# An encoder block on one core: rotary keys third among the column tiles, early sums of wo on ScalarE, and thirty products of zeros ahead of the last four

## The chip, the core and the metric

The kernel runs on one core of a Trainium2 chip. A core has TensorE (PE, matrix products into PSUM), VectorE (DVE), ScalarE (ACT), GpSimd (POOL) and SyncE (SP, which here issues nearly all DMAs). The metric is device time in microseconds, the median of several runs. One execution was also recorded by the hardware profiler; times inside the kernel come from that record and count from its first instruction.

## What is computed

One layer: a projection `x @ w_in` into eight groups of columns, two kinds of attention, a gate, an output projection, and LayerNorm on the residual. Cut to what matters:

```python
def reference(x, w_in, rel_pos_bias, sink_logits, w_out, ln_gain, ln_bias):   # x: (1, 1024, 1024) float32
    h = jnp.einsum('bsd,de->bse', x, w_in[layer])                             # 2688 columns
    q_a, k_a, v_a, z_a, q_b, k_b, v_b, z_b = jnp.split(h, SPLIT_POINTS, axis=-1)
    y_a = neighborhood_attention(q_a, k_a, v_a, rel_pos_bias[layer])          # 8 heads of 64, window 8 x 16
    y_b = windowed_gqa_with_sink(rotary(q_b), rotary(k_b), v_b, sink_logits[layer])   # 8 query, 2 key heads, |i-j| <= 128
    mixed = jnp.concatenate([y_a * jax.nn.silu(z_a), y_b * jax.nn.silu(z_b)], axis=-1)
    y = jnp.einsum('bse,ed->bsd', mixed, w_out[layer])
    x = layer_norm(DEEPNORM_ALPHA * x + y, ln_gain[layer], ln_bias[layer])
```

## The kernel before

Products of float32 matrices are formed from float16 parts: each operand is scaled by a power of two and split into a high and a low part, and three products (high x high, high x low, low x high) go into one PSUM bank. The scale of a matrix comes from sums of absolute values.

The work has four stages, and the order of all instructions is written out by the program itself (a manual schedule), so each engine's queue is exactly in program order.

1. **Values.** The value columns are projected first (L537), while `x` and the value weights arrive.
2. **Prologue of column tiles.** The other 21 tiles of 128 columns of `w_in` are named in `ORDER` (L30): `zb*` and `z*` are gates, `kb` the rotary keys, `qb*` rotary queries, `k*`, `q*` the other attention. `project(name)` runs two groups of 24 products (L430), one for each half of the 1024 tokens, each into one of two PSUM banks tagged `pj`. A group may start when the bank's last reader, two groups before, is done. After a group comes `evac`. The first six tiles (`NPRO`) are projected in a block, 288 products counted by `ran`; steps behind a group are hung at a count of products (`after=`, `at(...)`). For a rotary tile these are: a copy to `rp_raw` on ACT (L364), a shuffle, two products and a sum on DVE (L365 to L368), high parts on ACT (L300), low parts on DVE (L306), and for keys copies on POOL (L347). For the first three names of `ORDER` a gate's SiLU is one ACT instruction (L391); later gates take a tanh on ACT (L394) and a step on DVE (L395). Beside this stand the sums over the columns of the other 15 tiles (`sum_w`, L755, L757). `w_scale` turns sums into scales with a small product on PE (L266) and a chain of small DVE steps; its last call, at product 217, uses the sums of all 15.
3. **Attention loop.** 128 units, one a step: scores on PE (L860, L861), a biased minimum on DVE (L870), exp on ACT (L885), a split into high and low parts on ACT and DVE (L895, L896), a transposing DMA issued by SP (L899), and products with the values (L925). The remaining 15 tiles and then parts of the output projection fill PE between the scores (`FILL_AT`). Other work is put on ACT, DVE or POOL by a planner: each operation has a priority and a cost in us for each engine that may take it, `due` books the work of an engine, and an engine takes an operation where its booked work leaves room before the next step. The sums of `wo` (`wo_scan`, L968 on ACT or L970 on DVE) are such operations: 16 of them, through four buffers, so that the load of each waits for the sum four before. The first four are placed in the prologue on ACT, the others are queued at the steps in `SCAN_LD` (0, 2, 4, 6, ...). When all are done, `wo_scale` forms the scale of `wo` at a step from 24 on that is a multiple of four.
4. **Output projection and LayerNorm** (`final`). Eight blocks of 128 rows; products at L1178, sums into the residual and statistics on DVE (L1213, L1219). The last block ends in `norm_last`: part of its normalisation is done by PE, with `identf` times the bias first (L1243), then, when the row's scale is known, two diagonal matrices `dr` and `dn` made by ACT (L1248, L1249) times the row and the gain (L1250, L1251). At float32 each of these is recorded as two products.

Of the kernel before, what the change touches and what calls it, by code (L numbers as in the profile page):

```python
# [26 lines left out]
QSCALE = 2.0 ** -15  # L27
LTT, LPP, BH, ND, NA, NX, F1 = 1, 6, 9, 1, 1, 8, 0.2
NSPLIT, NP = 6, 2
ORDER = ["zb0", "z0", "zb1", "kb", "qb0", "z1", "qb1", "zb2", "qb2", "k0", "qb3", "zb3", "q0", "k1", "q1",  # L30
         "k2", "q2", "k3", "q3", "z2", "z3"]
NPRO = 6
NS = 21 - NPRO
NR = 5
FILL = ORDER[NPRO:]
FILL_AT = [0, 8, 17, 25, 33, 41, 49, 57, 66, 74, 82, 90, 98, 106, 113, 121, 123.5, 126, 128, 131, 136]
# [29 lines left out]
def hybrid_block(ctx, tc, xT, x, wt, wv, wo, bias, sink, gain, lbias, cos, sin, bmask, out):  # L66
    nc = tc.nc
# [10 lines left out]
    def bank(tag):  # L78
        bufs = {"pj": 2, "s": 4, "t": 2}[tag]
        return (ps1 if bufs == 1 else ps2).tile([128, 512], F32, tag=tag, name=f"ps_{tag}", bufs=bufs)  # L80
# [19 lines left out]
    def zslot(name, tag="z"):  # L100
        return zp.tile([128, S], F32, tag=tag, name=name, bufs=3 if tag == "z" else 1)
# [15 lines left out]
    invt = const.tile([128, 2], F32, name="invt")  # L117
    NT = len(ORDER)
    unit = const.tile([128, 2], F32, name="unit")
# [11 lines left out]
    warm = const.tile([128, 128], F16, name="warm")  # L131
# [17 lines left out]
    clock = {"step": None}  # L149
# [19 lines left out]
    def enq(eng, fn, *deps, prio=1, after=0, cost=None):  # L169
        op = Op(eng, fn, deps, prio, cost)  # L170
        if clock["step"] is not None:
            queues[eng].append(op)
        elif after:
            events.setdefault(ran[0] + after, []).append(op.emit)
        else:
            op.emit()
        return op
# [44 lines left out]

    NH = 2 * len(ORDER)
    NL = NH - 2 * NR
# [37 lines left out]
    def w_scale(n):  # L262
# [8 lines left out]
        nc.vector.tensor_scalar(v, g, xrs, 0.5, op0=ALU.mult, op1=ALU.mult)  # L271
        nk, nq = ORDER.index("kb"), ORDER.index("qb0")
        if n >= NPRO - 1:
# [60 lines left out]
    def split_k(p, half, src, dep=None):  # L334
        col = dep is None
        ops, high = [], []
        prio = 0 if dep is None else 1
        eng = "pool" if dep and clock["step"] is not None else "dve"
        for j in range(2):
            a, o = slice(64 * j, 64 * j + 64), slice(64 - 64 * j, 128 - 64 * j)  # L340
            hi, lo = split_hl(lambda j=j, a=a: place(own("kh", p, j), a, half, col),
                              lambda j=j, a=a: place(own("kl", p, j), a, half, col),
                              taken_from(src, a, col), dep is None, eng)

            def dup_(w, j=j, a=a, o=o):
                t = own(w, p, j)
                nc.gpsimd.tensor_copy(place(t, o, half, col), place(t, a, half, col))  # L347

            high.append((enq("act", hi, dep, prio=prio, after=28 if dep else 0), lo, dup_))
        for j, (o1, lo, dup_) in enumerate(high):  # L350
            o2 = enq(eng, lo, *([o1] if dep else [h[0] for h in high]), prio=prio, after=32 if dep else 0)
            ops.append(o2)
            dup = [enq("pool", lambda d=dup_: d("kh"), o1, after=32 if dep else 0, cost=0.62),
                   enq("pool", lambda d=dup_: d("kl"), o2, after=36 if dep else 0, cost=0.62)]
            stk_ops.setdefault((p, j, half), []).extend(dup)
        return ops

    def rope(ps, half):
        live = clock["step"] is not None
        sl = slice(512 * half, 512 * half + 512)  # L360
        eng, mul = ("pool", nc.gpsimd) if live else ("dve", nc.vector)
        raw = tiles["ap"].tile([128, 1024], F32, tag="va", name="rp_raw", bufs=6)[:, :512]
        sw = tiles["ap"].tile([128, 1024], F32, tag="va", name="rp_sw", bufs=6)[:, :512]
        o1 = enq("act", lambda: nc.scalar.activation(raw, ps, AF.Copy, scale=QSCALE), prio=0)  # L364
        o2 = enq("dve", lambda: nc.vector.stream_shuffle(sw, raw, SWAP), o1, after=2)  # L365
        o3 = enq(eng, lambda: mul.tensor_mul(raw, raw, tiles["cos"][:, sl]), o2, after=3)
        o4 = enq(eng, lambda: mul.tensor_mul(sw, sw, tiles["sin"][:, sl]), o2, after=3)
        o5 = enq(eng, lambda: mul.tensor_add(raw, raw, sw), o3, o4, after=4)  # L368
        return raw, o1, o5

    def evac(name, half, ps):
        sl = slice(512 * half, 512 * half + 512)
        kind = name.rstrip("0123")
        p = int(name[-1]) if name[-1].isdigit() else 0
        n = ORDER.index(name)
        if kind in ("kb", "qb"):
            raw, o1, o5 = rope(ps, half)
            if kind == "kb":
                split_k("b", half, raw, o5)
            else:  # L380
                split_q(f"b{p}", half, raw, o5)
            return [o1]
        if kind == "k":
            return split_k(p, half, ps)
        if kind == "q":
            return split_q(p, half, ps)
        e = 4 + p if kind == "zb" else p
        if half == 0:
            zt[e] = zslot(f"z{e}", ZTAG.get(name, "z"))
        if name in ORDER[:3]:  # L390
            nc.scalar.activation(zt[e][:, sl], ps, AF.Silu, scale=inv[:, n:n + 1])  # L391
            return []
        half_inv = invt[:, 0:1] if n < NPRO else invt[:, 1:2]
        o = enq("act", lambda: nc.scalar.activation(zt[e][:, sl], ps, AF.Tanh, scale=half_inv), prio=0)  # L394
        o2 = enq("dve", lambda: nc.vector.scalar_tensor_tensor(  # L395
            zt[e][:, sl], zt[e][:, sl], 1.0, ps, op0=ALU.add, op1=ALU.mult), o, prio=0)
        stk_ops.setdefault(name, []).append(o2)
        return [o2]
# [565 lines left out]
    def wo_scan(i, b):  # L964
        def scan(eng):
            m = wom[:, 4 * i + b:4 * i + b + 1]
            if eng == "act":
                nc.scalar.activation(junk2, wor[:, b], AF.Abs, accum_out=m)  # L968
            else:
                nc.vector.tensor_reduce(m, wor[:, b], axis=mybir.AxisListType.X, op=ALU.add, apply_absolute_value=True)  # L970

        scans.append(enq("any", scan, load_ops["wor", i, b], prio=1.9,
                         cost={"act": 0.85, "dve": 0.68} if clock["step"] is not None else {"act": 0.85}))

    for n in range(NSCAN):
        at(190 + 6 * n, wo_load, SCAN[n // 4], n % 4)
        at(222 + 8 * n, wo_scan, SCAN[n // 4], n % 4)
# [217 lines left out]
    def final():  # L1195
# [25 lines left out]
        def row_stats(t):  # L1221
            mv = fp.tile([128, 2], F32, tag="mv", name="mv")
            nc.vector.bn_aggr(mv, stats[t][:, :8 if t == 3 else 2, :])
            sd = fp.tile([128, 1], F32, tag="sd", name="sd")
            nc.scalar.activation(sd, mv[:, 1:2], AF.Sqrt, bias=eps)
            return mv, sd
# [13 lines left out]
        def norm_last(t):  # L1240
            ts = slice(128 * t, 128 * t + 128)
            xr = xrs[t]
            nc.tensor.matmul(pn[:, :WP], identf, bb[:, HP], start=True, stop=False)  # L1243
            mv, sd = row_stats(t)
            nc.vector.scalar_tensor_tensor(xr[:, H0], xr[:, H0], mv[:, 0:1], gb[:, H0], op0=ALU.subtract, op1=ALU.mult)
            rstd, nmr = row_scale(mv, sd)
            dr, dn = (fp.tile([128, 128], F32, name=n, bufs=1) for n in ("dr", "dn"))
            nc.scalar.activation(dr, identf, AF.Copy, scale=rstd)  # L1248
            nc.scalar.activation(dn, identf, AF.Copy, scale=nmr)  # L1249
            nc.tensor.matmul(pn[:, :WP], dr, xr[:, HP], start=False, stop=False)  # L1250
            nc.tensor.matmul(pn[:, :WP], dn, gb[:, HP], start=False, stop=True)  # L1251
            nc.vector.scalar_tensor_tensor(xr[:, H1], xr[:, H1], mv[:, 0:1], gb[:, H1], op0=ALU.subtract, op1=ALU.mult)
            nc.scalar.copy(xr[:, HP], pn[:, :WP])
            for h in (H0, H1):
                nc.vector.scalar_tensor_tensor(xr[:, h], xr[:, h], rstd, bb[:, h], op0=ALU.mult, op1=ALU.add)
                nc.sync.dma_start(out[ts, h], xr[:, h])
            nc.scalar.dma_start(out[ts, HP], xr[:, HP])
# [121 lines left out]
    for i in range(-LD, NU + LO):  # L1379
# [9 lines left out]
        if i in SCAN_LD:  # L1389
            n, b = divmod(NSCAN + SCAN_LD.index(i), 4)  # L1390
            wo_load(SCAN[n], b, *scans[-4:-3])
            wo_scan(SCAN[n], b)
# [7 lines left out]
        if i in B_LD:  # L1400
            n = B_LD.index(i)
# [145 lines left out]
```

## Time and profile before

| | |
|---|---|
| median of three runs | 446.61 us (445.05 to 447.45) |
| profiled execution | 444.73 us, its span 442.9 us |
| PE busy | 431.9 us, 97% of the span |
| DVE, ACT, POOL busy | 333.6, 313.7, 280.5 us |
| mean granted PE clock | 0.994 |

The span runs from the first to the last instruction; the execution's own time has some work of start and end around it. Busy times are unions of the recorded durations. A product is recorded for longer than the pipeline needs it, so rows of PE overlap: the distance from start to start tells the rate.

### The profile page before, as it was taken

The page shows a single profiled execution, that of the slowest core. Times are in us where ns is not written, and L with a number is a line of the kernel's source. Part 1 is how long each engine was busy: PE and PEld are TensorE (multiplying, and loading weights), DVE is VectorE, ACT ScalarE, POOL GpSimd, SP SyncE. Part 2 cuts the span into 40 slices and gives each one's busy share as a digit, 9 for nine tenths or more (in the row PEclk, how much of TensorE's full clock was granted, in tenths as well). Part 3 has the DMA queues.
Part 4 walks back from the last instruction along what each step waited for, and adds up shares of the span by engine and source line. Part 5 has one row for each costly group of instructions (what it writes and reads, how often), then busy time and mean ns, then how long its engine had stood idle before and what let it go on. Part 6 is the DMA issues. An engine that isn't in the chain of part 4 may idle for free.

```text
span 442.9 us, 9338 instructions
## 1 busy us (share of the span) xinstructions
PE 431.9 (97%) x3205; PEld 251.3 (57%) x3205; DVE 333.6 (75%) x821; ACT 313.7 (71%) x660; POOL 280.5 (63%) x299
## 2 busy tenths in 40 slices
PE   8999999999999999999999999999999999999992
PEld 7997754444445555565555565656556565444451
DVE  5978967519988898888888977878778756665554
ACT  5749789759678888888988969788788753342221
POOL 0120074535848647779998799798989871077681
PEclk9999999999999999999999999999999999999997
DMA  7922469995138999985969999999799979612122
GB/s 255 406 95 60 132 234 337 259 308 161 48 96 184 188 195 186 206 162 123 179 137 214 194 198 210 225 185 187 141 199 228 154 130 385 252 47 96 47 91 100
DMA packets 128815, 80.12 MB, mean 181 GB/s; under 512 B 97280, under 2 KB 106368, under 8 KB 128768
## 3 DMA queue, kind: packets, MB, share of 16 engines
q1 hardware_dynamic: 128624, 79.40, 74.5%
q8 instruction: 25, 0.41, 0.4%
q14 instruction: 22, 0.18, 0.1%
q10 hardware_dynamic: 144, 0.13, 0.1%
HBM read 48.01 MB, written 8.42 MB: 127 GB/s over the span
## 4 chain that ended last, share of the span: by engine, by line
PE 80%; DMA 6%; DVE 5%; issue 3%; POOL 2%; ACT 1%; SPq 1%; POOLq 0%; DVEq 0%; ACTq 0%
PE ps_pj L430 35%; PE ps_s L1178 9%; PE ps_t L925 7%; PE ps_s L537 6%; PE ps_pj L1178 4%; PE ps_s L860 4%; PE ps_s L861 4%; DMA vd<-vt 3%; PE ps_pj L537 3%; PE ps_t L537 3%; PE ps_t L1178 2%; DMA ws<-in_wt 2%; PE ps_t L948 2%; POOL wl L246 1%; DMA wvraw<-in_wv 1%
## 5 line engine op out<-in xcount | busy, mean ns | idle before, releaser
L430 PE MATMUL ps_pj<-xf,wh 128*128 128x512 f16 x672 | 201.3, 379 | 1.1 <-DVE z L395 1.1
L430 PE MATMUL ps_pj<-xf,wl 128*128 128x512 f16 x336 | 127.3, 379 | 0.0
L430 PEld LDWEIGHTS <-wh 128*128 128x128 f16 x672 | 63.7, 98 | 61.0 <-issue 1.3
L885 ACT ACTIVATE ps_s<-sn,nm 128x385 f32<-128x385 f32 (+3 forms) x128 | 70.9, 554 | 32.5 <-DVE nm L870 32.2
L896 DVE SCALAR_TENSOR_TENSOR split<-ps_s,split 128x384 f16<-128x384 f32 (+1 forms) x128 | 66.8, 522 | 19.3 <-ACT split L895 17.7
L245 POOL TENSOR_SCALAR wr<-wr,wsc 128x512 f32<-128x512 f32 x32 | 23.8, 744 | 65.2 <-ACT wh L240 56.1
L895 ACT ACTIVATE split<-ps_s 128x384 f16<-128x384 f32 (+1 forms) x128 | 58.2, 454 | 1.6
L430 PEld LDWEIGHTS <-wl 128*128 128x128 f16 x336 | 32.8, 98 | 38.1
L870 DVE CUSTOM_DVE_ANT_0 sn<-ps_s,bias,sg 128x368 f32<-128x368 f32 (+1 forms) x64 | 36.2, 566 | 13.8 <-PE ps_s L861 13.8
L870 DVE CUSTOM_DVE_ANT_0 sn<-ps_s,bm,nsk 128x384 f32<-128x384 f32 (+1 forms) x64 | 40.7, 636 | 2.4 <-PE ps_s L861 2.2
L246 POOL TENSOR_TENSOR wl<-wr,wh 128x512 f16<-128x512 f32 x32 | 39.6, 1238 | 2.7
L860 PE MATMUL ps_s<-ks,qs 128*128 128x384 f16 (+2 forms) x128 | 39.7, 310 | 0.0
L861 PE MATMUL ps_s<-ks,qs 128*128 128x384 f16 (+2 forms) x128 | 39.7, 310 | 0.0
L925 PEld LDWEIGHTS <-tr 128*128 128x128 f16 (+1 forms) x1056 | 36.2, 98 | 2.4
L1178 PEld LDWEIGHTS <-A 128*128 128x128 f16 x216 | 20.1, 98 | 20.7
L347 POOL COPY ks<-ks 64x512 f16<-64x512 f16 x40 | 26.5, 662 | 5.8 <-DVE ks L306 1.8
L1213 DVE SCALAR_TENSOR_TENSOR xr<-ps_s,yc,xr 128x512 f32<-128x512 f32 (+1 forms) x22 | 16.0, 727 | 14.5 <-PE ps_s L1178 14.0
L1281 ACT ACTIVATE xr<-xr,nmr,rstd 128x1024 f32<-128x1024 f32 x6 | 7.4, 1240 | 27.0 <-POOL nmr L1232 27.0
L240 ACT ACTIVATE wh<-wr,wsc 128x512 f16<-128x512 f32 x32 | 22.8, 712 | 0.7 <-DVE wsc L270 0.7
L1178 PEld LDWEIGHTS <-m 128*128 128x128 f16 x144 | 13.9, 98 | 15.8
L537 PEld LDWEIGHTS <-xf 128*128 128x128 f16 x192 | 18.6, 98 | 7.2
L1283 POOL TENSOR_TENSOR xr<-xr,gb 128x512 f32<-128x512 f32 x13 | 16.8, 1290 | 8.3 <-ACT xr L1281 8.1
(214 smaller groups left out, 892.3 us busy)
## 6 DMA issues: line engine op xcount, KB each, us to landing
wr<-in_wt SPq DMA_DIRECT2D x32, 256.0 KB, 3.6
ws<-in_wt SPq DMA_DIRECT2D x15, 512.0 KB, 7.2
wor<-in_wo SPq DMA_DIRECT2D x20, 256.0 KB, 3.8
xr<-in_x SPq DMA_DIRECT2D x8, 512.0 KB, 10.6
out<-xr SPq DMA_DIRECT2D x15, 256.0 KB, 2.0
wob<-in_wo SPq DMA_DIRECT2D x14, 256.0 KB, 3.8
bias<-in_bias SPq DMA_DIRECT2D x8, 440.0 KB, 4.4
wvraw<-in_wv SPq DMA_DIRECT2D x9, 320.0 KB, 5.7
```

The lines of the kernel that those rows point to most:

```text
L246: nc.gpsimd.tensor_sub(l, raw, h)
L347: nc.gpsimd.tensor_copy(place(t, o, half, col), place(t, a, half, col))
L430: nc.tensor.matmul(ps, a[:, k % 4, :], mv, start=(k == 0 and i == 0), stop=(k == KT - 1 and i == 2))
L537: nc.tensor.matmul(ps[:, :320], lh[:, ts], rh[:, cs], start=(k == ko[0] and i == 0), stop=(k == ko[-1] and i == 2))
L860: nc.tensor.matmul(ps[:, :n], q, sl[0], start=True, stop=False)
L861: nc.tensor.matmul(ps[:, :n], q, sl[1], start=False, stop=True)
L870: nc.vector.tensor_tensor_reduce(sn[:, :n], ps[:, :n], bias_t, sg[:, c:c + 1], init, op0=ALU.add, op1=ALU.min, accum_out=nm)
L885: nc.scalar.activation(pt[:, :m], sn[:, :m], AF.Exp, bias=nm, scale=-1.0, accum_out=acc)
L895: nc.scalar.activation(hl[:, :m, 0, :], src, AF.Copy, scale=PSCALE)
L896: nc.vector.scalar_tensor_tensor(hl[:, :m, 1, :], src, PSCALE, hl[:, :m, 0, :], op0=ALU.mult, op1=ALU.subtract)
L925: nc.tensor.matmul(ps[:, w * m:w * m + e], a, b_, start=(i == 0), stop=(i == len(mms) - 1))
L1178: nc.tensor.matmul(ps[:, cs], lh[:, 128 * t:128 * t + 128], rh[:, cs], start=(fresh and e == 0 and n == 0), stop=(e == len(terms) - 1 and ...
```

## The change

Three edits. The rotary keys `kb` change places with the gate tile `zb1`; the condition for the SiLU form of a gate becomes its index below 4, so that `zb1` in fourth place keeps it. The sums of `wo` that are queued at the loop's steps 0, 2 and 4 may go to ACT alone; before, every sum queued inside the loop could go to ACT or DVE. In `norm_last`, thirty products of a 128 x 128 float16 tile of zeros with itself, into a bank that nothing reads, are put on PE between the product with the bias and the four that wait for `dr` and `dn`.

```diff
-ORDER = ["zb0", "z0", "zb1", "kb", "qb0", "z1", "qb1", "zb2", "qb2", "k0", "qb3", "zb3", "q0", "k1", "q1",
+ORDER = ["zb0", "z0", "kb", "zb1", "qb0", "z1", "qb1", "zb2", "qb2", "k0", "qb3", "zb3", "q0", "k1", "q1",
          "k2", "q2", "k3", "q3", "z2", "z3"]
...
-        if name in ORDER[:3]:
+        if n < 4:
             nc.scalar.activation(zt[e][:, sl], ps, AF.Silu, scale=inv[:, n:n + 1])
             return []
...
         scans.append(enq("any", scan, load_ops["wor", i, b], prio=1.9,
-                         cost={"act": 0.85, "dve": 0.68} if clock["step"] is not None else {"act": 0.85}))
+                         cost={"act": 0.85, "dve": 0.68} if (clock["step"] or 0) > 4 else {"act": 0.85}))
...
             nc.tensor.matmul(pn[:, :WP], identf, bb[:, HP], start=True, stop=False)
+            busy = bank("s")
+            for _ in range(30):
+                nc.tensor.matmul(busy[:, :128], warm, warm, start=True, stop=True)
             mv, sd = row_stats(t)
```

## The prediction

> **What bounds the kernel now.** I read the page first (shares, the clock row, the chain), then the waits of TensorE (PE), then the timeline around each wait.
>
> ```profile
> span 442.9 us, 9338 instructions
> ...
> PE 431.9 (97%) x3205; PEld 251.3 (57%) x3205; DVE 333.6 (75%) x821; ACT 313.7 (71%) x660; POOL 280.5 (63%) x299
> ...
> PE 80%; DMA 6%; DVE 5%; issue 3%; POOL 2%; ACT 1%; SPq 1%; POOLq 0%; DVEq 0%; ACTq 0%
> ```
>
> PE is busy for 431.9 of 442.9 us, and the chain that ended last is 80% PE. So a change can only pay where PE waits, and can only cost where it makes PE wait or gives it more work on the path. The waits of PE are four (who waited for whom: us in total, times, longest):
>
> ```profile
> PE ps_t L1250 <- ACT dr L1248: 2.7, 1, 2.7
> PE ps_pj L430 <- DVE z L395: 1.1, 1, 1.1
> PE ps_t L463 <- DVE warm L132: 1.0, 1, 1.0
> PE ps_pj L537 <- ACT wvh L493: 0.7, 1, 0.7
> ```
>
> The last two lie at the start, which the diff does not touch. The second is the hand-over from the prologue (six column tiles) to the attention loop, where the order of tiles matters. The first is the wait in `norm_last`, where the thirty products go. Everything from 123.5 us to the last rows is one unbroken stream of PE, so the sums of wo have no PE wait to remove.
>
> **Part 1: rotary keys third instead of fourth.** The wait that it can touch, in the timeline (start, us taken, engine, line, what, and in brackets the idle time before it and who ended it):
>
> ```profile
> 122.04 0.27 PE L860 MATMUL ps_s<-ks,qs 128*128 128x256 f16 x1
> ...
> 122.15 0.27 PE L861 MATMUL ps_s<-ks,qs 128*128 128x256 f16 x1
> ...
> 122.78 0.69 DVE L395 SCALAR_TENSOR_TENSOR z<-z,ps_pj 128x512 f32<-128x512 f32 x1
> ...
> 123.52 0.59 PE L430 MATMUL ps_pj<-xf,wh 128*128 128x512 f16 x2 [1.10 <-DVE z L395]
> ```
>
> PE wants the accumulator bank of z1's first half; VectorE (DVE) reads it at L395 only until 123.47. Counted from start to start, L861 is followed after 1.37 us, where L860 was followed after 0.11: the wait costs 1.26 us. L395 is late because DVE's queue ahead of it has no gap from 109.63 on:
>
> ```profile
> 107.79 1.81 DVE L306 TENSOR_TENSOR ks<-rp_raw,ks 64x512 f16<-64x512 f32 x2
> 109.63 0.17 DVE L267 TENSOR_REDUCE wg<-ps_t 128x1 f32<-128x15 f32 x1
> ...
> 111.97 0.73 DVE L365 STREAM_SHUFFLE rp_sw<-rp_raw 128x512 f32<-128x512 f32 x1
> ...
> 115.39 1.40 DVE L306 TENSOR_TENSOR ks<-rp_raw,ks 64x512 f16<-64x512 f32 x2
> ...
> 116.82 0.73 DVE L365 STREAM_SHUFFLE rp_sw<-rp_raw 128x512 f32<-128x512 f32 x1
> ...
> 120.12 2.63 DVE L306 TENSOR_TENSOR qs<-rp_raw,qs 64x512 f16<-64x512 f32 x2
> ```
>
> The two `ks` rows are the low parts of kb, the tile that moves. All of kb's steps hang at fixed counts of products behind its own two groups (shuffle 2, products 3, sum 4, high parts 28, low parts 32, copies 32 and 36), so they all move with it by one tile: 48 products, some 10.4 us at the 0.216 us of this stream (starts at 123.52 and, two products on, 123.95). That takes the 1.40 us out of the queue directly ahead of L395: 123.47 becomes 122.07, just ahead of the 122.26 at which PE could go on. The 1.81 us also leaves, so the scale chain at 109.63 need not start that late: it waits only for PE's row at 106.69 (below), and the rotary work behind it, of 3.4 and 3.3 us, only for PE's groups. L395 can then run as early as its tanh allows, and the wait goes with room to spare. What replaces kb in fourth place is zb1, whose evacuation is one ScalarE (ACT) SiLU per half and nothing on DVE or POOL; with `n < 4` it keeps that SiLU. **Minus 1.26 us.**
>
> What does kb's new place collide with? Its high parts (four casts on ACT), its copies (POOL) and its rotary steps (DVE) now stand among the last sums over w's columns, and PE itself waits for these sums: the small product L266 stands in PE's own queue, so everything behind it would wait too.
>
> ```profile
> 95.98 1.06 ACT L755 ACTIVATE junk<-ws 128x1024 bf16<-128x1024 f32 x1 [3.58 <-DMA ws<-in_wt]
> ...
> 103.14 0.72 ACT L240 ACTIVATE wh<-wr,wsc 128x512 f16<-128x512 f32 x1 [0.70 <-DVE wsc L270]
> ...
> 105.89 0.19 ACT L755 ACTIVATION_READ_ACCUMULATOR junk<-ws 128x1 f32 x1
> ```
> ```profile
> 106.69 0.17 PE L266 MATMUL ps_t<-wm,ones 128*128 128x15 bf16 x1
> ```
> ```profile
> L300 ACT CAST ks<-rp_raw 64x512 f16<-64x512 f32 x4 | 2.4, 610 | 0.1
> L364 ACT ACTIVATE rp_raw<-ps_pj 128x512 f32<-128x512 f32 x4 | 2.3, 581 | 0.0
> L391 ACT ACTIVATE z<-ps_pj,inv 128x512 f32<-128x512 f32 x2 | 1.4, 687 | 1.5 <-PE ps_pj L430 1.4
> ```
>
> (The last three are groups: busy us, mean ns of one.) The last sum ends at 106.08, PE comes at 106.69: 0.61 us of room. In program order all four casts now come ahead of it. The first two (about 1.2 us) fall into the 3.58 us in which ACT waits for a load. The other two add 2 x 0.61 = 1.22; two SiLU in place of two copies to rp_raw add 2 x 0.106 = 0.21; the 0.70 us at L240 goes, since DVE no longer has kb's first rotary ahead of that scale. Net 0.73 us later, so PE waits 0.12. Ends: 0 (all hidden) and, with all four casts and both SiLU in full and the 0.70 kept, 2.44 + 0.21 - 0.61 = 2.04. I take 0.12, because the gap of 3.58 us is three times what is put into it. **Plus 0.12 us.**
>
> The other users of kb come later than before relative to it: the first scores at 122.04 only find their keys earlier. rp_raw and rp_sw lie over tiles of the value weights, with which the prologue is done long before, so they wait for nothing; SP's queue is passed by none of kb's steps, since kb issues no DMA of its own.
>
> **Part 2: sums 4 to 6 of wo on ACT alone.** The rows of these sums:
>
> ```profile
> L968 ACT ACTIVATE junk<-wor x10: 612/622/630, 109.6 to 194.6; 128x512 bf16<-128x512 f32 x10
> L968 ACT ACTIVATION_READ_ACCUMULATOR junk<-wor x10: 186/188/192, 110.2 to 195.2; 128x1 f32 x10
> ...
> L970 DVE TENSOR_REDUCE wom<-wor x6: 679/684/687, 143.1 to 174.4; 128x1 f32<-128x512 f32 x6
> ```
> ```profile
> ACT ps_s L885 <- DVE nm L870: 10.8, 13, 2.1
> ```
>
> Each group has its fewest, middle and most ns, and the first and last start. DVE's first two (from 143.1) are sums 4 and 5 (of 0 to 15), queued at steps 0 and 2; sum 6 is on ACT already. So two of 0.684 leave DVE and two of 0.62 + 0.19 = 0.81 enter ACT, which from 120 to 200 us waits 10.8 us for DVE: ACT has the room, DVE gains what ACT was waiting for. PE does not wait in this stretch, so the direct gain is 0. A sum that slips holds back the load of the sum four later (same buffer) and behind it SP's queue; the sums 8 and 9 are queued four steps after 6 and more, so I expect them, and the scale of wo, at the same steps. **0 us**; ends: minus 0, since nothing waits, and plus 1.6 (both sums in full on PE's path).
>
> **Part 3: thirty products in the wait.**
>
> ```profile
> 431.90 0.50 PE L1178 MATMUL ps_s<-wo,z 128*128 128x128 f16 x6
> ...
> 432.91 0.65 PE L1243 MATMUL ps_t<-bb,identf 128*128 128x256 f32 x2
> 436.27 0.67 PE L1250 MATMUL ps_t<-xr,dr 128*128 128x256 f32 x2 [2.71 <-ACT dr L1248]
> 436.78 0.59 PE L1251 MATMUL ps_t<-gb,dn 128*128 128x256 f32 x2
> ```
> The stretch after them, by windows (length, busy of PE, its weight loads, DVE, ACT and POOL, the granted clock, DMA), and the first products of the program:
>
> ```profile
> 434.30:437.70 3.40, 1.10 (x4) 0.68 (x4) 3.15 (x8) 0.99 (x3) 0.00 (x0) 1.00 0.20 77
> 437.70:441.00 3.30, 0.00 (x0) 0.00 (x0) 0.00 (x0) 0.37 (x1) 0.00 (x0) 0.50 0.40 150
> ```
> ```profile
> 0.99 2.95 PE L463 MATMUL ps_t<-warm 128*128 128x128 f16 x26 [0.99 <-DVE warm L132]
> ```
>
> Six 128-wide f16 products take 0.50 us, from 431.90 to 432.24 start to start, or 0.056 each. Thirty take 1.7 us, from about 433.4 to 435.1, and `dr` releases PE at 436.27: they lie wholly inside the wait, with 1.1 us left. Their bank is one that the third row block used and DVE has long read. At the slow rate of the first 26 (2.95 us, about 0.107 each) they would take 3.2 and overrun by 0.3 to 0.5; PE comes from a full-clock stream, so I leave that out. In this profile the granted clock was 1.00 up to 437.70: the last four products already ran at full clock, and all that is left to save is the refill of the first (0.67 us for the first two, 0.59 for the last two): **minus 0.08 us.** But the clock fell to 0.50 at 437.70, right behind a stretch of 3.40 us of which 1.10 were busy. A run in which such a boundary lies 1 to 2 us earlier would run these four products at half rate.
>
> The Trainium skill, "TensorE: Matmul & The Clock Gate", Part 1 (The HAM clock gate), says that the clock halves after a window of about 3.4 us that was idle, and that the windows run freely, not with the kernel. By that rule read strictly, a wait of 2.7 us holds no whole idle window and the zeros are worth nothing in any run: the sum would lose no term but the chance of the first rival below. The trace disagrees with the strict reading: the stretch ahead of the fall was a third busy.
>
> **The sum.** Minus 1.26, plus 0.12, plus 0, minus 0.08: minus 1.22 us. The profiled execution took 444.73 us (its span of 442.9 and 1.83 around it), so it would take 443.5. The median of the runs before, 446.61 (445.05 to 447.45), lies 1.88 above it; the same 1.22 taken from it gives **445.4 us**, 0.27% faster, inside the 0.5% that a measurement of this kernel can tell from no change.
>
> **The rivals.**
>
> *The clock falls in the wait in most runs.* The profile is faster than all three timed runs; in those the boundary may lie inside the wait, and the last four products then take about twice as long, as the first 26 of the program do beside those of L1178 (0.107 against 0.056). One of the four takes some 0.215 (0.59 for two, less the 0.38 for which one lasts): 4 x 0.215 = 0.86 us, straight on the path to the last output. The zeros end that. Time: 446.61 - 1.22 - 0.86 = 444.5. For it: the fall behind a window one third busy. Against it: of 3.4 us of possible positions only some 1.5 hit the four products.
>
> *Slower: the sums over w wait behind kb's casts.* If the load of the tenth sum comes earlier, or the rotary work later, so that the casts miss the gap of 3.58 us, PE waits 2.04 us at L266. The wait at L395 goes all the same, so the time is 446.61 + 2.04 - 1.26 - 0.08 = 447.3. It turns from gain to loss when the last sum ends later than 106.69 + 1.34 = 108.0 us.
>
> *The gain is given back inside attention.* PE comes 1.2 us earlier to every tile that it reads; where a transposed tile lands shortly before use, PE waits instead, and the two sums on ACT push exp, split and transfer back by up to 1.6. Then 446.6, no change. For it:
>
> ```profile
> 266.65 2.69 SPq L899 DMA_TRANSPOSE tr<-split  x2
> ```
> ```profile
> 271.02 0.85 PE L925 MATMUL ps_t<-va,tr 128*128 128x64 f16 x22
> ```
> ```profile
> tr<-split SPq DMA_TRANSPOSE x128, 3.6
> ```
>
> PE reads such tiles 4.4 us after the issue, and landing takes a median of 3.6. Against it: the front of the pipeline starts earlier too, as DVE is rid of its backlog at 123.
>
> **How the numbers follow.** Forecast 0.45, clock rival 0.30, given back 0.14, slower rival 0.11. The runs of before differ by 2.4 us, so a new median may lie 1 us off. The bound for faster is 444.38: the clock rival is beyond it 7 times in 10 at most with that scatter and a somewhat larger saving (0.21), the forecast 4 times in 10 (0.18), the others hardly (0.01): 0.40. The bound for slower is 448.84: the slower rival with the scatter, or an order that the planner changes further on: 0.10. That leaves 0.50. The range goes from the clock rival less the scatter, 443.3, to the slower rival, 447.4.
>
> **What would show it.** Right: no PE wait for L395; kb's casts ahead of 95.98; DVE's scale chain at 107 instead of 109.6; L266 at most 0.3 late; no sum of wo on DVE before 150; thirty products of 0.056 and a wait for `dr` of about 1.1. Wrong: PE waits at L266 of over 1 us, new waits for `tr` at L925 or for banks at L860, the scale of wo a step of four later, or thirty products at 0.107.

## The result, and the profile after

Median of 11 runs: 442.56 us (441.67 to 444.87), against 446.11 us (444.57 to 447.48) for 11 runs of the kernel before on the same chip. The ratio is 0.993, with a 95% interval of 0.9913 to 0.9947: 3.1 us faster by the ratio (3.55 by the two medians), where 1.2 were forecast, and below the forecast range. The profiled execution took 441.67 us.

The page of the changed kernel:

```profile
span 439.9 us, 9401 instructions
...
PE 433.5 (99%) x3235; PEld 253.7 (58%) x3235; DVE 335.0 (76%) x820; ACT 314.2 (71%) x662; POOL 279.4 (64%) x299
...
PE 97%; DVE 2%; ACT 0%; issue 0%; DVEq 0%; ACTq 0%
```

The thirty products are the thirty more on PE; ACT has two records more and DVE one fewer. The chain that ended last was 80% PE, with 6% of DMA and 5% of DVE; now it is 97% PE. The waits of PE (who for whom: us in total, times, longest):

```profile
PE ps_t L1253 <- ACT dr L1251: 1.3, 1, 1.3
PE ps_t L463 <- DVE warm L132: 1.0, 1, 1.0
```

The wait for DVE's L395 is gone, and no new one has come. The wait for `dr` is 1.3 because zeros fill the rest. (From L1243 on, line numbers are three higher.)

The hand-over to the loop, in the timeline of the changed kernel:

```profile
118.95 0.69 DVE L395 SCALAR_TENSOR_TENSOR z<-z,ps_pj 128x512 f32<-128x512 f32 x1
...
121.48 0.27 PE L861 MATMUL ps_s<-ks,qs 128*128 128x256 f16 x1
121.59 0.59 PE L430 MATMUL ps_pj<-xf,wh 128*128 128x512 f16 x2
```

L395 is 3.83 us earlier than its 122.78, so PE goes on 0.11 us after L861 instead of 1.37. That is the 1.26 us of the forecast.

The end is where the rest lies. The last steps in the kernel before, in the timeline (ACTq: ACT's sequencer issuing a DMA):

```profile
436.04 0.39 ACT L1249 ACTIVATE dn<-identf,nmr 128x128 f32<-128x128 f32 x1
437.75 0.37 ACT L1253 COPY xr<-ps_t 128x256 f32<-128x256 f32 x1 [1.32 <-PE ps_t L1251]
438.15 2.05 ACTq L1257 DMA_DIRECT2D out<-xr  x1
```

and in the changed kernel:

```profile
431.08 0.65 PE L1243 MATMUL ps_t<-bb,identf 128*128 128x256 f32 x2
431.57 1.84 PE L1246 MATMUL ps_s<-warm 128*128 128x128 f16 x30
434.71 0.67 PE L1253 MATMUL ps_t<-xr,dr 128*128 128x256 f32 x2 [1.30 <-ACT dr L1251]
435.22 0.60 PE L1254 MATMUL ps_t<-gb,dn 128*128 128x256 f32 x2
435.90 0.37 ACT L1256 COPY xr<-ps_t 128x256 f32<-128x256 f32 x1 [1.05 <-PE ps_t L1254]
436.31 0.37 ACTq L1260 DMA_DIRECT2D out<-xr  x1
```

The issue of the same 128 KB write takes 0.37 us instead of 2.05. Laid side by side, start to start:

| stretch | before | after | difference, us |
|---|---|---|---|
| to the first product of the column tiles | 59.64 | 58.95 | -0.69 |
| to the first L861 | 62.51 | 62.53 | +0.02 |
| from it to the next L430 | 1.37 | 0.11 | -1.26 |
| to the product with the bias | 309.39 | 309.49 | +0.10 |
| to the first product with `dr` | 3.36 | 3.63 | +0.27 |
| to ACT's copy of the result | 1.48 | 1.19 | -0.29 |
| to the start of ACT's last issue | 0.40 | 0.41 | +0.01 |
| to the end of the span | 4.75 | 3.59 | -1.16 |

They add up to 3.0 us, the difference of the spans. The first row is no effect of the change: it lies ahead of all three edits, and over the profiles below it varies from 58.69 to 59.94. So this pair of profiles shows 2.3 us that can belong to the change, against the 3.1 by the ratio. What is left to explain is the last row, and the +0.27 and -0.29 above it.

While the long issue ran, the DMA queues carried a packet of instructions beside the data. Kernel before, 438.10 to 440.30, the stretch of that issue (packets, MB, share of 16 engines; then the DMA issued there, with the time to its landing):

```profile
q14 instruction: 1, 0.01, 1.4%
...
out<-xr ACTq DMA_DIRECT2D x1, 128.0 KB, 3.5
```

The changed kernel has that packet between 434.0 and 436.3, while ACT issues nothing, and its write lands sooner:

```profile
q14 instruction: 1, 0.01, 1.2%
```
```profile
out<-xr ACTq DMA_DIRECT2D x1, 128.0 KB, 2.3
```

A packet of that queue brings 8 KB of program: by the page of either kernel, 22 of them are 0.18 MB. ACT's compiled program has 842 instructions before, 53,888 bytes or 64 each, and 846 after, so a packet holds 128. Seven packets of the queue are ACT's by their spacing: in the kernel before they come when ACT has begun 58, 192, 323, 450, 575, 707 and 834 of its records (its sequencer's included), 125 to 134 apart. The 22 packets together hold 2816 instructions, more than ACT has, so the queue serves other engines too. In both kernels the last of ACT's comes at the same place of its program: 834 records are begun in the kernel before, and the 834th is the last DMA issue; 833 are begun in the changed one, where the last issue is the 838th. My theory (the fetch theory) was that a piece of program, fetched while the DMA is being issued, lengthens the issue, and that ACT's program had only to become longer by two instructions or more. The chain of the work that ended last shows a second mark of the same place, in the kernel before ahead of ACT's copy (start, us, what):

```profile
437.39 0.02 issue
437.41 0.02 ACTq L1253
437.43 0.32 issue
437.75 0.37 ACT xr L1253
```

and in the changed kernel ahead of `sd`:

```profile
433.32 0.32 issue
433.64 0.30 ACT sd L1225
```

"issue" is time in which the engine waited for nothing that the profile shows. In both the 0.32 us stand ahead of ACT's 832nd record, so a fixed distance ahead of the fetch; they explain both small rows of the table, -0.29 at the copy and +0.27 at `dr`.

### The profile page after: what moved, and what is told of

It reads as the page before. It is cut to its first block, busy times and chain, and to the rows that moved or that the text cites. A ratio compares the mean times of both kernels' runs of the same rounds, so it can differ in the third digit from the quotient of the medians.

```text
span 439.9 us, 9401 instructions
## 1 busy us (share of the span) xinstructions
PE 433.5 (99%) x3235; PEld 253.7 (58%) x3235; DVE 335.0 (76%) x820; ACT 314.2 (71%) x662; POOL 279.4 (64%) x299
## 4 chain that ended last, share of the span: by engine, by line
PE 97%; DVE 2%; ACT 0%; issue 0%; DVEq 0%; ACTq 0%
PE ps_pj L430 49%; PE ps_s L1178 9%; PE ps_t L925 7%; PE ps_s L537 6%; PE ps_pj L1178 4%; PE ps_s L860 4%; PE ps_s L861 4%; PE ps_pj L537 3%; PE ps_t L537 3%; PE ps_t L1178 2%; PE ps_t L948 2%; PE ps_t L463 1%; DVE stats L1219 1%; DVE xr L1213 1%; DVE xr L1281 0%
## 5 line engine op out<-in xcount | busy, mean ns | idle before, releaser
L430 PE MATMUL ps_pj<-xf,wh 128*128 128x512 f16 x672 | 201.5, 379 | 0.0
L430 PE MATMUL ps_pj<-xf,wl 128*128 128x512 f16 x336 | 127.5, 379 | 0.0
L430 PEld LDWEIGHTS <-wh 128*128 128x128 f16 x672 | 63.7, 98 | 59.8
L245 POOL TENSOR_SCALAR wr<-wr,wsc 128x512 f32<-128x512 f32 x32 | 22.9, 717 | 65.2 <-ACT wh L240 59.9
L430 PEld LDWEIGHTS <-wl 128*128 128x128 f16 x336 | 32.9, 98 | 38.1
L861 PE MATMUL ps_s<-ks,qs 128*128 128x384 f16 (+2 forms) x128 | 39.7, 310 | 0.0
L1178 PEld LDWEIGHTS <-A 128*128 128x128 f16 x216 | 20.2, 98 | 20.7
L1178 PEld LDWEIGHTS <-m 128*128 128x128 f16 x144 | 13.9, 98 | 15.8
## 6 DMA issues: line engine op xcount, KB each, us to landing
xr<-in_x SPq DMA_DIRECT2D x8, 512.0 KB, 10.5
```

The costliest lines, as they stand in the source:

```text
L430: nc.tensor.matmul(ps, a[:, k % 4, :], mv, start=(k == 0 and i == 0), stop=(k == KT - 1 and i == 2))
L861: nc.tensor.matmul(ps[:, :n], q, sl[1], start=False, stop=True)
L1178: nc.tensor.matmul(ps[:, cs], lh[:, 128 * t:128 * t + 128], rh[:, cs], start=(fresh and e == 0 and n == 0), stop=(e == len(terms) - 1 and ...
```

## The experiments

Three questions were open: which edit brings which part, whether the fetch theory holds, and whether the zeros bring anything. Ratios are to the kernel before on the same chip, with 95% intervals; the three sets of kernels that ran together are e1 to e4, e5 to e8 and e9 to e12.

**Each edit alone, and two copies of one number.** e1 has only the first edit:

```diff
-ORDER = ["zb0", "z0", "zb1", "kb", ...
+ORDER = ["zb0", "z0", "kb", "zb1", ...
...
-        if name in ORDER[:3]:
+        if n < 4:
```

> Only the rotary keys are moved (with the SiLU condition). ACT's program grows from 842 to 844 instructions. Fetch theory: besides the wait for L395 (1.26 us) the whole change won about 1.2 us net because ACT's block of instructions that was loaded during its last DMA issue (2.05 us for that issue) is now loaded earlier, and ACT's length decides this. Then this kernel gains both: 2.3 to 2.8 us, and the last ACT issue takes about 0.4 us. Clock theory: the zeros won the rest, by the clock; then this kernel gains 1.3 us, and the last ACT issue still takes 2 us.

Measured: 441.84 us, 0.9936 [0.9921, 0.9950], the whole gain. Its waits of PE:

```profile
PE ps_t L1250 <- ACT dr L1248: 2.7, 1, 2.7
PE ps_t L463 <- DVE warm L132: 1.0, 1, 1.0
PE ps_t L266 <- ACT junk L260: 0.3, 1, 0.3
```

and its end:

```profile
434.73 0.99 PE L1250 MATMUL ps_t<-xr,dr 128*128 128x256 f32 x2 [2.71 <-ACT dr L1248]
435.51 1.06 PE L1251 MATMUL ps_t<-gb,dn 128*128 128x256 f32 x2
436.66 0.37 ACT L1253 COPY xr<-ps_t 128x256 f32<-128x256 f32 x1 [1.79 <-PE ps_t L1251]
437.06 0.37 ACTq L1257 DMA_DIRECT2D out<-xr  x1
```

No wait for L395, and an issue of 0.37: with the keys alone ACT's program has 844 instructions. The two more do no work; the trace has them as two waits for a semaphore at L300, the casts of the keys, where the kernel before has none. Two smaller things show: PE waits for the sums of w at L266 (0.3 by this view; the mechanism of my slower rival, at a fraction of its price), and the four last products run at half rate from 434.94 on, 1.84 us from first start to last end instead of 1.10.

e2 has only the second edit:

```diff
-                         cost={"act": 0.85, "dve": 0.68} if clock["step"] is not None else {"act": 0.85}))
+                         cost={"act": 0.85, "dve": 0.68} if (clock["step"] or 0) > 4 else {"act": 0.85}))
```

> Only the sums of wo queued at steps 0, 2 and 4 go to ACT alone. ACT's program grows from 842 to 844 instructions. Fetch theory: 1.0 to 1.5 us faster, all of it behind the last product, with the last ACT issue at about 0.4 us; the wait for L395 stays at 1.1 us. Clock theory: no change (within 0.3 us), the last ACT issue still 2 us.

Measured: 443.35 us, 0.9968 [0.9955, 0.9981]. The wait for L395 stays, yet it is 1.4 us faster than before:

```profile
PE ps_pj L430 <- DVE z L395: 1.4, 1, 1.4
```
```profile
439.27 0.37 ACTq L1257 DMA_DIRECT2D out<-xr  x1
```

One sum more on ACT is two instructions more (844), and the issue is short.

e3 has only the thirty products (ACT at 842).

```diff
+            busy = bank("s")
+            for _ in range(30):
+                nc.tensor.matmul(busy[:, :128], warm, warm, start=True, stop=True)
```

> Only the thirty products of zeros are added. ACT's program stays at 842 instructions. Fetch theory: 0.1 us faster in the profile (the refill of the first of four products), at most 0.5 in the median of runs, the last ACT issue still 2 us. Clock theory: 1.2 us or more faster, the last ACT issue at 0.4 us.

Measured: 445.52 us, 1.0013 [1.0000, 1.0026]: no gain. The issue is long:

```profile
440.25 2.00 ACTq L1260 DMA_DIRECT2D out<-xr  x1
```

Its profiled execution also lost 3.0 us between the start of the loop and the product with the bias, ahead of its edit; 1.3 of them are three waits for transposed tiles inside attention, which no other profile in the order of before has.

e4 is the kernel before with two ACT copies that nothing needs, at the start of the output stage (844 instructions). None of the three edits is in it.

```diff
         nc.vector.memset(eps, EPS)
+        pad = fp.tile([128, 1], F32, name="pad", bufs=1)
+        for _ in range(2):
+            nc.scalar.copy(pad, eps)
```

> The kernel before with two copies of one number a partition on ACT at the start of the output stage, read by nothing; ACT is idle there. ACT's program grows from 842 to 844 instructions, nothing else changes. Fetch theory: 1.0 to 1.5 us faster, the last ACT issue at about 0.4 us. Clock theory: no change, or 0.2 us slower, the last ACT issue still 2 us.

Measured: 443.91 us, 0.9980 [0.9969, 0.9990]. Work was added that serves nothing, and the kernel became 0.9 us faster by the ratio:

```profile
437.99 0.37 ACTq L1260 DMA_DIRECT2D out<-xr  x1
```

The profile also shows the copies' own cost: PE waits of 0.3 and 0.2 us at L1178 for tiles that ACT and DVE make there. From the start of the loop to the product with the bias it takes 310.46 us where the kernel before takes 309.39.

**All three edits, without zeros, and with ACT's length put back.** e5 is the changed kernel unaltered, for comparison on the same chip.

> The changed kernel itself, as the measure for the three others of this call. Fetch theory with both other terms: 0.6 to 0.8% faster than before, last ACT issue 0.4 us, the four last products 1.1 us.

Measured: 442.06 us, 0.9935 [0.9918, 0.9953]; issue 0.37.

e6 is the changed kernel without the thirty products.

> The changed kernel without the thirty products (keys and sums moved; ACT stays at 846 instructions). Theory that the zeros pay only when a boundary of the clock falls into the wait: in a profile the four last products take either 1.1 us or 1.8 to 2.0; the median of runs is 0.2 to 0.6 us above that of the changed kernel. Theory that the zeros do nothing: no difference. Theory that the zeros won the tail: 1.2 us above, with a last ACT issue of 2 us.

Measured: 442.21 us, 0.9936 [0.9919, 0.9952]. In the median nothing separates it from e5, in the profile something does. Windows of e6 (length, busy of PE, weight loads, DVE, ACT and POOL, the granted clock, DMA):

```profile
431.26:434.67 3.41, 1.01 (x12) 0.60 (x9) 2.99 (x11) 0.29 (x1) 1.61 (x2) 1.00 0.24 94
434.67:438.08 3.41, 2.05 (x4) 1.18 (x4) 1.95 (x5) 1.07 (x3) 0.00 (x0) 0.50 0.28 103
```

The same windows of the changed kernel:

```profile
431.26:434.67 3.41, 2.15 (x32) 1.83 (x31) 2.99 (x11) 0.80 (x3) 1.08 (x2) 1.00 0.21 79
434.67:438.08 3.41, 1.10 (x4) 0.68 (x4) 1.43 (x3) 0.56 (x2) 0.00 (x0) 1.00 0.41 153
```

Without zeros PE was busy for 1.01 of 3.41 us and the clock fell to 0.50 right behind, so the four products took 2.05 us; with them it was busy for 2.15, the clock stayed and they took 1.10.

e7 has the keys moved, one of the four sums in the prologue given to DVE, and no zeros, so that ACT is back at 842. e8 is the changed kernel with two of those sums on DVE and one copy that nothing needs, also 842, zeros kept. The sums of e7, against the changed kernel:

```diff
-                         cost={"act": 0.85, "dve": 0.68} if (clock["step"] or 0) > 4 else {"act": 0.85}))
+                         cost={"act": 0.85, "dve": 0.68} if clock["step"] is not None else
+                         {"dve": 0.68} if b > 2 else {"act": 0.85}))
```

> Only the rotary keys are moved, and one of the four sums of wo in the prologue is done by DVE in place of ACT (DVE has room there), which brings ACT's program back to 842 instructions. Fetch theory: the last ACT issue is 2 us again and only the wait for L395 is won, so 1.0 to 1.6 us faster than before, some 1.2 us slower than with the keys moved alone. If the keys' move itself won the tail: 2.5 to 3 us faster.

> The changed kernel with two of the four sums of wo in the prologue on DVE in place of ACT and one copy of one number a partition on ACT at the start of the output stage: ACT's program is back at 842 instructions. Fetch theory: the last ACT issue takes 2 us again, and the kernel is 1.2 us slower than the changed one; PE still does not wait for L395. Otherwise: equal to the changed kernel.

Measured: e7 443.51 us, 0.9963 [0.9951, 0.9975]; e8 443.80 us, 0.9977 [0.9963, 0.9991]. Neither waits for L395; both have the long issue again. e7:

```profile
437.57 2.06 ACTq L1258 DMA_DIRECT2D out<-xr  x1
```

e8:

```profile
438.23 2.18 ACTq L1263 DMA_DIRECT2D out<-xr  x1
```

In both windows of those issues lies one packet of the instruction queue. e8 is 1.7 us slower than e5 beside it; some of that is its own, PE waiting 0.4 us for a sum ahead of L266 and 0.3 for a tile in the output stage. From the product with the bias to the end of the span e8 takes 10.2 us and e5 8.8.

**ACT's length by a whole fetch.** e9 to e11 are the changed kernel with copies that nothing needs, spread over the output stage behind the scalings and normalisations of the row blocks:

```diff
             nc.scalar.activation(xrs[t], xrs[t], AF.Copy, scale=ALPHA)
+            if t in (5, 2, 6, 3, 7):
+                pads(2)
```

(`pads(n)` issues `n` of the copies of e4.) e9 brings ACT to 857, e10 to 970 and e11 to 974: 842 + 128 and 846 + 128.

> The changed kernel with fourteen more ACT copies of one number a partition, spread over the output stage behind the scalings of blocks 5, 2, 6, 3 and 7 and behind the normalisations, where ACT has room: ACT's program goes from 846 to 857 instructions. Fetch theory: the piece of program that ACT fetches near its end, and the pause of 0.32 us that stood three records ahead of it (in the changed kernel's profile ahead of sd, 433.32 to 433.64), now come eleven instructions earlier, out of the last row block. So the last issue takes 0.37 us as in the changed kernel, and sd starts 0.3 earlier, the wait for dr is 1.0 instead of 1.3, and the time is 0.3 us under the changed kernel's: ratio to the kernel before 0.9925 to 0.9935. Rival, the pause belongs to sd's wait and not to the fetch: it stays, ratio 0.993 to 0.995. Rival, the copies cost what they take: 14 times 0.2 us somewhere on the path, ratio near 0.998.

> The changed kernel with the same copies, but so many (11 or 12 at each place, 130 asked for) that ACT's program has 970 instructions: 842 + 128, and a fetched piece holds 128. Fetch theory: the last DMA issue of ACT stands again where it stood in the kernel before, so an instruction fetch falls into it and the issue takes about 2.0 us instead of 0.37; the last write lands some 3.5 us behind its issue instead of 2.3, and the run is 1.2 to 1.7 us slower than the kernel with 974. Rival, the length of ACT's program has nothing to do with it and the copies of the earlier experiments moved something else: the issue takes the same in this kernel and in that with 974, and their times agree within 0.5 us. What the copies themselves cost (some 2.3 us of ACT at each place, which has 3 to 8 us idle in each 10) is the same in both.

> The changed kernel with such copies up to 974 instructions of ACT, 846 + 128. Fetch theory: the fetch comes four instructions ahead of the place that it has with 970, no DMA is being issued then, the issue takes 0.37 us, and the run is 1.2 to 1.7 us faster than the kernel with 970. The rival: the two agree within 0.5 us.

Measured: e9 441.78 us, 0.9926 [0.9908, 0.9945]; e10 447.71 us, 1.0050 [1.0032, 1.0067]; e11 447.24 us, 1.0045 [1.0030, 1.0060]. The last issue of e10, and the instruction queue between 441.2 and 443.3:

```profile
441.29 1.89 ACTq L1270 DMA_DIRECT2D out<-xr  x1
```
```profile
q14 instruction: 1, 0.01, 1.9%
```

and that of e11:

```profile
443.31 0.37 ACTq L1270 DMA_DIRECT2D out<-xr  x1
```

128 instructions on, the long issue is back, and four more take it away: the period of the fetch, as the theory said. In e10 the packet comes when 962 records of ACT are begun, 128 more than in the kernel before. In e11 its place is not the one that I expected: the nearest packet comes at 425.26, with 947 begun, amid the extra copies and 18 us ahead of the last issue. In e10 the copy of the result, too, starts 0.37 us after the last product and in e11 0.09, as before and after. From the product with the bias to the end of the span, e10 takes 10.5 us and e11 9.1. The times do not differ by the 1.2 to 1.7 that I expected: 0.5, with overlapping intervals, which by time alone is what the rival said. In the profiles e11 comes to the product with the bias 2.4 us later; 1.6 of these are there at the start of the loop, and in the output stage PE waits more for the extra copies:

e10:

```profile
PE ps_s L1178 <- DVE xr L1223: 2.9, 3, 2.2
```

e11:

```profile
PE ps_s L1178 <- DVE xr L1223: 4.0, 3, 2.6
```

So the two show what the length of ACT's program does to the issue and to the end of the profile, but their times do not show its worth. In e9 the pause ahead of `sd` is gone and the wait for `dr` is 1.0 instead of 1.3, as expected, but 0.3 us is too little for the intervals: e9 is not told apart from the changed kernel, and no version of the twelve is shown to beat it.

e12 is the changed kernel with the sums of wo as before.

> The changed kernel with the sums of wo as before (sums 4 and 5 may go to VectorE again): keys and zeros alone, 844 instructions of ACT. If the second edit is worth nothing by itself: the issue takes 0.37 us (844 as in the kernel with the keys alone), no wait for L395, and the ratio is the changed kernel's, 0.9925 to 0.995. Rival, the sums on ACT carry part of the gain through VectorE in the loop: the ratio is 0.996 or more, with waits of PE between 123 and 433 us that the changed kernel's profile does not have.

Measured: 441.69 us, 0.9920 [0.9905, 0.9935], no wait of PE but the two of the changed kernel. Without the second edit nothing is lost that these intervals could show.

**Together.** Sorted by what the profile shows at L395 and at the last issue:

| | issue of 2.0 to 2.2 us | issue of 0.37 us |
|---|---|---|
| PE waits for L395 | before 1; e3 1.0013 | e2 0.9968, e4 0.9980 |
| no wait for L395 | e7 0.9963, e8 0.9977 | changed 0.993, e1 0.9936, e5 0.9935, e6 0.9936, e9 0.9926, e12 0.9920 |

(e10 and e11 are left out: their copies cost 5 us.) Against the kernel before, the means are 0.9974 for the issue alone, 0.9970 for the wait alone and 0.9931 for both: 1.2, 1.3 and 3.1 us. The two parts add up to 2.5; the 0.6 missing are within the intervals (each is some 0.6 us to either side), and e4 and e8 carry waits of their own. The profiles split the same way: from the product with the bias to the end of the span, the five with the long issue (e10 among them) take 10.0 to 10.7 us, and the nine others 8.5 to 9.3.

## Why the prediction was wrong, and where it was right

**Keys third: right in kind and size.** The wait of 1.26 us is gone with room to spare, and the medians of e7 and e8 give 1.3 for it. The scale chain, at 109.63 before, now starts at 106.23, earlier than the 107 I named. The forecast cost was L266, 0.12. In the timeline of the changed kernel:

```profile
91.98 1.25 ACT L300 CAST ks<-rp_raw 64x512 f16<-64x512 f32 x2
95.37 1.06 ACT L755 ACTIVATE junk<-ws 128x1024 bf16<-128x1024 f32 x1 [2.14 <-DMA ws<-in_wt]
...
98.97 1.24 ACT L300 CAST ks<-rp_raw 64x512 f16<-64x512 f32 x2
...
105.79 0.19 ACT L755 ACTIVATION_READ_ACCUMULATOR junk<-ws 128x1 f32 x1
```

The gap of 3.58 us took two casts and is 2.14, as I reckoned; the other two come behind the sum that starts at 95.37, though I had named all four ahead of it. The last sum ends at 105.98 and PE comes at 106.03: the room of 0.61 was used up but for 0.05. In five of the ten profiles with the keys third PE waits there: 0.2 to 0.4 us in e1, e7, e8 and e11 by the view of waits (0.6 to 0.8 counted from start to start over both products of L266), and 0.5 in e6 by that count alone. So the term of 0.12 was too small in half of them, and the 2.04 of the slower rival far too large.

**Sums of wo: right at nothing, wrong in the steps.** I expected none on DVE before 150 us; one stood there:

```profile
148.06 0.69 DVE L970 TENSOR_REDUCE wom<-wor 128x1 f32<-128x512 f32 x1 [0.57 <-DMA wor<-in_wo]
```

ACT has one sum more than before, not two. PE waited for none of it, and e12 shows no loss without the edit.

**Zeros: the rates right, the worth open.** Thirty took 1.84 us, and all four products ran at full clock, as they did in the profile before. The rival in which the clock falls inside the wait is a real mechanism: in e1, e2, e6 and e7 it fell, and the four took 1.74 to 2.05 us. Of six profiles without zeros (with that of before) that is four, of the eight with zeros none. But the two pairs that differ in the zeros alone, e5 with e6 and e12 with e1, differ by 0.0001 and 0.0016, both inside the intervals; and the zeros alone (e3) brought nothing. Part of the cost of the half clock comes back at the end: the last write lands 1.8 us behind its issue in e1, e2 and e6 and 2.3 in the other profiles with a short issue. From the product with the bias to the end of the span e6 takes 9.3 us and e5 8.8. So the zeros are worth somewhere from nothing to about 1 us, and these runs do not say more.

The Trainium skill, "TensorE: Matmul & The Clock Gate", Part 1 (The HAM clock gate), lets the clock halve after an idle window of about 3.4 us. The traces agree with the half (0.50) and not with a window that must be idle: the one of 3.41 us ahead of the fall in e6 holds 1.01 us of products.

**The step that failed** is the sum itself. It took the profiled execution, subtracted what changes on PE, and so held everything behind the last product as given, down to "all that is left to save is the refill of the first". The issue of the last write lay there with 2.05 us, on the path of the last thing that the kernel does. My own window 437.70 to 441.00 covered it; I read its clock and not its DMA. I costed the edits by the time that their instructions take, and not by what two more of them do to the place of everything behind them in ACT's program. That term, 1.2 us of 3.1 by the medians (0.9 in e4, 1.7 between e8 and e5), is as large as the one that I had. The clock rival, 444.5, came nearer to the measured time than the forecast did, but by a cause that brought nothing in e3.

**What stays open.** That the long issue comes with the fetch and returns after 128 instructions is shown. Why a fetch lengthens an issue is not: whether the issue has to wait for its own next instruction or the transfer's descriptors stand behind the packet, no run here tells. Nor is shown whether ACT's earlier fetches, which meet no DMA issue of its own, cost anything.

## What to carry to other kernels

Read the last DMA issue like a wait: when it ends the program and takes five times what another run of the same code takes, the difference is on the path, and an instruction packet in its window is a reason to move it by a few instructions. When an edit of a few instructions gains more than its wait, add as many that do nothing to the unchanged kernel; if that gains as well, the edit's idea is not what paid. Cost an edit on the last path to the end of its write, not to the end of its last product.

## What the runs showed of the hardware

An instruction fetch in ACT's last DMA issue costs time (0.37 against 1.9 to 2.2 us in every profile). SP's issues, too, are longer when they meet a fetch, but that of another engine. In the kernel before, of the transposing issues recorded singly:

```profile
144.72 2.00 SPq L899 DMA_TRANSPOSE tr<-split  x1
...
150.71 1.21 SPq L899 DMA_TRANSPOSE tr<-split  x1
...
155.99 1.19 SPq L899 DMA_TRANSPOSE tr<-split  x1
```

Within the first lies one packet of the other instruction queue (16 KB each; 25 of them are 0.41 MB). That queue is PE's: from one packet to the next PE's records, weight loads included, advance by 254 in the mean, and 16 KB are 256 instructions of 64 bytes. Over all 14 profiles, of the 1363 transposing issues with no instruction packet in their time none took over 1.8 us; of the 241 with a packet of 16 KB 133 did; of the 188 with a packet of 8 KB alone 2 did. No run tested this by moving a packet, and it says that an issue can become longer without its own engine's fetch.

The Trainium skill, "Runtime: NRT & Kernel Launch", Instruction fetch mechanics, gives blocks of 16 KiB and calls the cost of crossing one mostly hidden. The 16 KB of PE's packets agree; ACT's place repeats with 8 KB, and where its fetch meets its last DMA issue it is not hidden: 1.5 to 1.8 us longer.

Second, the pause of 0.32 us on ACT, at a fixed place ahead of the fetch, which the profile puts down to nothing at all. Third, work that does nothing can gain: two copies of one number a partition took 0.9 us off (e4).
